# The second block's gates of tiles 4 to 7: pairs of weight tiles by seven quarter products

## The chip, the cores and the metric

The kernel runs on one core of one Trainium2 chip, in one launch. Time is the device time of that launch in microseconds. TensorE (PE), VectorE (DVE), ScalarE (ACT) and GpSimd (POOL) each work through a queue of their own in order; SyncE (SP) starts most DMAs.

## The reference, cut to what matters

The program computes two transformer blocks on 512 tokens of 1024 features, in float32. The first block is one layer with attention, a recurrence and a mixture of experts. The second block has two layers, each a mixing layer and a feed-forward stage. The change touches the mixing layer:

```
h = rmsnorm(x, norm_mix_g[l])
proj = einsum('bsd,de->bse', h, w_in[l])          # q, k, v, retention, convolution, gate_pre
...
gates = sigmoid(gate_pre + b_gate[l]).reshape(B, S, 3, D)
y = (gates[:, :, 0] * (o_da @ w_branch_da[l]) + gates[:, :, 1] * (o_ret @ w_branch_ret[l])
     + gates[:, :, 2] * (o_sc @ w_branch_sc[l]))
x = x + y @ w_out[l]
```

`gate_pre` has 3 x 1024 features, each a sum over the 1024 features of `h`. The feed-forward stage that follows is `x + (silu(conv(h @ w_g)) * (h @ w_u)) @ w_out`, with 2816 features in the middle.

## The kernel before, in words

**Numbers in two halves.** A float32 matrix product is made of three matmuls in the chip's faster rounded format. Each operand is split into a high half, a copy by ACT (`split`, line 953), and a low half, the difference that DVE takes; `mm3` (line 929) adds high x high, high x low and low x high in PSUM. So each weight that is loaded costs an ACT copy and a DVE subtraction before PE can use it, and each product three matmuls per 128 features.

**The plain product.** `mm_fm` (line 1106) makes 128 output features for all 512 tokens: the weight chunk of 1024 x 128 is loaded and split (`load_w`, line 974), and for each of 8 groups of 128 input features three matmuls of 512 columns (tokens) follow, 24 in all. With `halves=2` it does the tokens in two halves of 256 columns, 48 matmuls. `x` is what `norm_fm` (line 988) leaves: the normalized activations, transposed, features on partitions, split.

**The seven products.** The feed-forward stage has another way. `norm_quarters` (line 1007) leaves the same activations in quarters: two halves of the features by two halves of the tokens. `token_sums` (line 1037) forms four sums and differences of these quarters: four 1024-wide additions of high and low half on POOL, four 1024-wide additions or subtractions on DVE, and a split of each result (ACT and DVE). They stay in SBUF for the whole stage. `mm_seven` (line 1060) takes two weight tiles at once, forms four differences of their quarters on DVE, splits seven weight quarters, and makes both output tiles from seven products of a quarter by a quarter, where the direct way needs eight; each product is 4 x 3 matmuls of 256 columns. Results of products are copied out of PSUM (`ea`, `eb`, `ec`) between further products, and three additions on DVE put the outputs together.

**The mixing layer.** `mix2` (line 1874) normalizes, then projects q, k and v, then weaves the attention with the convolution branch (`sc2`, six plain products) and the retention's projections, then the retention with the gates of tiles 0 and 1. What is left runs tile by tile, here called the tail: for feature tile j the three gates that are still missing (one per branch b, plain products, with a tanh on ACT), then the three branch products and their sum, `y`. The output product `mm_tm_res` ends the layer. In 24 gate products per layer and the six of `sc2`, `x` is the moving operand of 512 columns; the projections use it as the stationary one, 128 tokens at a time.

**What sets the order.** The program is recorded first and then ordered by a planner (`Prog.order`, line 592). It fills each engine's queue in an order of its own, with costs of operations, room in SBUF and the program's order as the priority: an operation may stand well ahead of its place in the program where its inputs are there and room is free. SBUF is a few segments, `f` and `wf` for float32 and `r`, `wr` and at times `s` and `t` for the rounded format. With the program's `swing` in the mixing layer (line 1911), `t` becomes rounded too; `wr`, `r`, `s` and `t` then have 37120 columns. `SHARES` (line 2253) holds stretches of the program, by number of operation, where the planner sets part of the room aside.

In all profiles every instruction carries line 346, where the planner emits it; names are those of the segments, `bank` is a PSUM bank.

Of the kernel before, what the change touches and what calls it, by code (L numbers as in the profile page):

```python
# [16 lines left out]
AF = mybir.ActivationFunctionType  # L17
# [159 lines left out]
class Engine:  # L177


    def __init__(self, prog, name):  # L180
        self._p, self._n = prog, name
# [5 lines left out]
class Prog:  # L187
# [289 lines left out]
    def plan(self):  # L477
# [3 lines left out]
        deps, share = self.preds, np.ones(len(self.ops) + 1)  # L481
        for i, k in SHARES:
            share[max(0, i - 600):i + 100] -= 0.05 * k
# [418 lines left out]
                self.left[b.live][head:b.last + 1] += b.n  # L902


class Kernel:
    def __init__(self, p, a, out, dbg=None):
        self.p = self.nc = p
# [198 lines left out]
    def mm_fm(self, src, x, kts=8, halves=1):  # L1106

        w = self.load_w3(src, kts, P)
        ps = self.ps()
        n = S // halves  # L1110
        for h in range(halves):
            sl = slice(h * n, (h + 1) * n)
            for j in range(kts):
                self.mm3(ps[:, sl], (w[0][:, j, :], w[1][:, j, :]), (x[0][j][:, sl], x[1][j][:, sl]), j == 0, j == kts - 1)
        return ps
# [758 lines left out]
    def mix2(self, l):  # L1874
        nc, a = self.nc, self.a
        F = lambda name, shape: self.t(shape, F32, name)
        lam_init = 0.8 - 0.6 * math.exp(-0.3 * l)
        x = self.norm_fm(a[f"g_mix2{l}"], "h")
        vec = self.load(a[f"vec2{l}"], [P, NVEC2], "vec2")
        hb = F("hbg", (P, 24))  # L1880
        self.ts(hb, vec[:, L2_GATE:L2_GATE + 24], 0.5, OP.mult)
# [18 lines left out]
        gates = {}  # L1900

        def gate(*js):
            for j, b in js:
                ps = self.mm_fm(a[f"w_gate{l}"][8 * b + j], x)
                g = gates[j, b] = F("gate", (P, S))
                self.act(g, ps, AF.Tanh, scale=0.5, bias=hb[:, 8 * b + j:8 * b + j + 1])
                yield
        self.weave((ret, 240), (gate(*((j, b) for j in range(2) for b in range(3))), 160))
        tiles = lambda z, n: [[z[q][:, k, :] for k in range(n)] for q in range(2)]
        oda, ort, osc = tiles(oda, 4), tiles(ort, 2), [[osc[k][q][:, 0, :] for k in range(2)] for q in range(2)]  # L1910
        self.p.swing({"t": "R"})
        y = []
        for j in range(8):
            self.run_all(gate(*((j, b) for b in range(3) if (j, b) not in gates)))
            gt = [gates[j, b] for b in range(3)]
            for b, (w, o, kts) in enumerate((("w_bda", oda, 4), ("w_bret", ort, 2), ("w_bsc", osc, 2))):
                ps = self.mm_fm(a[f"{w}{l}"][j], o, kts)
                self.stt(gt[b], gt[b], 1.0, ps, OP.add, OP.mult)
            self.tt(gt[0], gt[0], gt[1], OP.add)
            self.tt(gt[0], gt[0], gt[2], OP.add)  # L1920
            yh, yl = self.t([P, S], R32, "yh"), self.t([P, S], R32, "yl")
            self.act(yh, gt[0], AF.Copy, scale=0.5)
            self.stt(yl, gt[0], 0.5, yh.bitcast(F32), OP.mult, OP.subtract)
            y.append((yh, yl))
# [325 lines left out]
SCRATCH = {"rel": [4, 640], "hx": [S, D], "fold0": [P, P], "fold1": [P, P], "fold2": [P, P], "fold3": [P, P]}  # L2250
GE = 4
GROUP, PLAIN = 4, 2
SHARES = ((3749, 1), (11237, 1), (14294, 1))


def build(nc, tc, a, out, dbg=None, stop=None, start=None):
# [18 lines left out]
```

## Time and profile before

| what | value |
|---|---|
| time, median of 3 runs | 2387.47 us (2382.23 to 2387.71) |
| profiled execution | 2380.74 us, its span 2379.0 us |
| busy in the span | PE 2277.1, PE weight loads 1803.6, DVE 1527.9, ACT 950.9, POOL 82.0 us |
| mixing layers of the second block | about 780 to 1200 us and 1570 to 2000 us |
| their tails (tiles 2 to 7 and the output product) | about 1045 to 1200 us and 1840 to 2000 us |
| feed-forward stages | about 1225 to 1570 us and 2020 to 2375 us |

A busy time of PE counts rows whose ends are modelled and overlap the next row, so PE can read busy and still not start matmuls as closely as it could; the distance between starts tells more. "Granted clock" is the share of TensorE's full clock that the chip allowed. A wait names the engine, and the segment it wrote, that came last before an instruction could start.

### The profile page before, as it was taken

The page shows a single profiled execution, that of the slowest core. Times are in us where ns is not written, and L with a number is a line of the kernel's source. Part 1 is how long each engine was busy: PE and PEld are TensorE (multiplying, and loading weights), DVE is VectorE, ACT ScalarE, POOL GpSimd, SP SyncE. Part 2 cuts the span into 40 slices and gives each one's busy share as a digit, 9 for nine tenths or more (in the row PEclk, how much of TensorE's full clock was granted, in tenths as well). Part 3 has the DMA queues.
Part 4 walks back from the last instruction along what each step waited for, and adds up shares of the span by engine and source line. Part 5 has one row for each costly group of instructions (what it writes and reads, how often), then busy time and mean ns, then how long its engine had stood idle before and what let it go on. Part 6 is the DMA issues. An engine that isn't in the chain of part 4 may idle for free.

```text
span 2379.0 us, 35153 instructions
## 1 busy us (share of the span) xinstructions
PE 2277.1 (96%) x13578; PEld 1803.6 (76%) x13578; DVE 1527.9 (64%) x3521; ACT 950.9 (40%) x1609; POOL 82.0 (3%) x107
## 2 busy tenths in 40 slices
PE   7999969899999899999999999999999999999999
PEld 6767647644444776778889999978777888999998
DVE  7876573533222957553579888776664446988885
ACT  5445422121311534333336555443442334555542
POOL 0100010000100000100010000000010000100000
PEclk9979987879999999999999999999999999999999
DMA  5002232379997321122413333332111332232231
GB/s 198 19 19 59 69 95 105 138 270 406 355 378 298 115 80 37 54 98 81 141 55 107 107 106 100 116 132 86 39 58 48 125 114 99 81 98 95 101 116 45
DMA packets 87425, 287.87 MB, mean 121 GB/s; under 512 B 11060, under 2 KB 16308, under 8 KB 87256
## 3 DMA queue, kind: packets, MB, share of 16 engines
q1 hardware_dynamic: 84376, 275.12, 33.1%
q0 software_dynamic: 2880, 10.49, 1.2%
q8 instruction: 107, 1.75, 0.3%
q14 instruction: 62, 0.51, 0.1%
HBM read 281.10 MB, written 4.47 MB: 120 GB/s over the span
## 4 chain that ended last, share of the span: by engine, by line
PE 83%; DVE 10%; DMA 3%; ACT 2%; issue 2%; POOL 0%; ACTq 0%; SPq 0%; DVEq 0%; POOLq 0%
PE bank L346 83%; DVE seg_f L346 3%; DVE seg_t L346 2%; DVE seg_tiny L346 2%; DVE seg_s L346 1%; DVE seg_wr L346 1%; DMA seg_wf<-in_w_o 1%; ACT seg_f L346 1%; DVE seg_r L346 1%; DMA seg_f<-in_w_ffi 0%; ACT seg_wr L346 0%; DMA seg_r<-in_w_moe 0%; DMA seg_t<-in_rot 0%; DVE seg_wf L346 0%; ACT seg_t L346 0%
## 5 line engine op out<-in xcount | busy, mean ns | idle before, releaser
L346 PE MATMUL bank<-seg_r,seg_wr 128*128 128x512 f32 (+1 forms) x1706 | 436.0, 352 | 0.6 <-DVE seg_wr L346 0.3
L346 PEld LDWEIGHTS bank<-seg_r,seg_wr 128*128 128x128 f32 x1706 | 290.6, 190 | 45.5 <-issue 1.4
L346 PE MATMUL bank<-seg_s,seg_wr 128*128 128x256 f32 (+1 forms) x1134 | 309.0, 327 | 0.0
L346 PE MATMUL bank<-seg_wr 128*128 128x512 f32 (+2 forms) x922 | 260.8, 389 | 4.3 <-DVE seg_wr L346 3.1
L346 ACT ACTIVATE seg_f<-bank 128x256 f32<-128x256 f32 (+5 forms) x313 | 135.7, 438 | 262.5 <-PE bank L346 238.2
L346 PE MATMUL bank<-seg_t,seg_wr 128*128 128x256 f32 (+1 forms) x1176 | 235.6, 283 | 0.4 <-ACT seg_t L346 0.4
L346 PE MATMUL bank<-seg_wr,seg_r 128*128 128x512 f32 (+1 forms) x748 | 230.1, 393 | 2.7 <-DVE seg_r L346 1.7
L346 ACT ACTIVATE seg_wr<-seg_f 128x1024 fp32r<-128x1024 f32 (+2 forms) x178 | 163.1, 923 | 135.5 <-PE bank L346 94.4
L346 PEld LDWEIGHTS bank<-seg_s,seg_wr 128*128 128x128 f32 x1134 | 195.7, 191 | 19.7 <-DVE seg_t L346 0.2
L346 PEld LDWEIGHTS bank<-seg_wr 128*128 128x128 f32 x922 | 170.9, 194 | 47.7 <-issue 6.9
L346 PE MATMUL bank<-seg_wr,seg_s 128*128 128x512 f32 x610 | 206.4, 394 | 0.5 <-DVE seg_f L346 0.5
L346 PEld LDWEIGHTS bank<-seg_t,seg_wr 128*128 128x128 f32 x1176 | 186.0, 190 | 1.7 <-ACT seg_t L346 0.6
L346 PE MATMUL bank<-seg_s 128*128 128x512 f32 (+4 forms) x672 | 180.4, 370 | 1.1 <-DVE seg_t L346 1.1
L346 PE MATMUL bank<-seg_r,seg_s 128*128 128x512 f32 (+2 forms) x548 | 174.2, 380 | 2.2 <-ACT seg_f L346 1.9
L346 DVE TENSOR_TENSOR seg_f<-bank,seg_f 128x512 f32<-128x512 f32 (+4 forms) x212 | 128.7, 613 | 72.5 <-PE bank L346 64.3
L346 DVE TENSOR_TENSOR seg_f<-seg_f 128x512 f32<-128x512 f32 (+5 forms) x271 | 158.1, 597 | 23.0 <-ACT seg_f L346 16.6
L346 ACT ACTIVATE seg_wr<-seg_wf 128x1024 fp32r<-128x1024 f32 (+4 forms) x118 | 113.1, 964 | 131.7 <-PE bank L346 93.4
L346 PEld LDWEIGHTS bank<-seg_wr,seg_r 128*128 128x128 f32 x748 | 137.9, 188 | 34.4 <-DVE seg_f L346 2.4
L346 PE MATMUL bank<-seg_s,seg_r 128*128 128x512 f32 (+3 forms) x502 | 160.7, 383 | 0.3 <-ACT seg_r L346 0.3
L346 PE MATMUL bank<-seg_t,seg_s 128*128 128x256 f32 (+7 forms) x566 | 128.2, 333 | 16.2 <-DVE seg_f L346 10.0
L346 PE MATMUL bank<-seg_f 128*128 128x128 f32 (+6 forms) x971 | 117.3, 279 | 27.1 <-DVE seg_f L346 22.4
L346 PE MATMUL bank<-seg_r 128*128 128x512 f32 (+2 forms) x426 | 140.0, 375 | 1.0 <-ACT seg_f L346 1.0
(340 smaller groups left out, 3834.4 us busy)
## 6 DMA issues: line engine op xcount, KB each, us to landing
seg_s<-in_w_moe SPq DMA_DIRECT2D x58, 512.0 KB, 10.1
seg_f<-in_w_ffi SPq DMA_DIRECT2D x52, 512.0 KB, 3.4
seg_f<-in_w_moe SPq DMA_DIRECT2D x42, 512.0 KB, 9.6
seg_r<-in_w_moe SPq DMA_DIRECT2D x42, 512.0 KB, 10.2
seg_wf<-in_w_ffi SPq DMA_DIRECT2D x36, 512.0 KB, 3.4
seg_t<-in_w_moe SPq DMA_DIRECT2D x33, 512.0 KB, 10.1
seg_f<-in_w_ffo SPq DMA_DIRECT2D x30, 512.0 KB, 3.2
seg_f<-in_w_gate SPq DMA_DIRECT2D x29, 512.0 KB, 3.9
```

Of the source, the lines that this page charges most:

```text
L346: return self.chain(eng, f(*[self.place_of(v) for v in a], **{n: self.place_of(v) for n, v in k.items()}))
```

## The change

The mixing layer takes its normalized activations from `norm_quarters` in place of `norm_fm`. A view, `Quarters`, shows the quarters as the eight feature groups that the old code expects; a slice of tokens must lie within one half, so `mm_fm` on such an `x` always works in halves of 256 columns. The gates of tiles 0 to 3 stay plain products. The gates of tiles 4 to 7 are made two tiles at a time by `mm_seven`, three calls (one per branch) for tiles 4 and 5 and three for 6 and 7, in each of the two layers; the tanh works in place on the two results. The token sums that this needs are made from the quarters after the `swing` in the program. `SHARES` has other entries.

```
+class Quarters:
+    def __getitem__(self, q):
+        return [Row([self.z[i][k // 4][q][:, k % 4, :] for i in range(2)]) for k in range(8)]
+class Row:
+    def __getitem__(self, at):
+        sl = at[1]
+        i = sl.start // 256
+        return self.halves[i][:, sl.start - 256 * i:sl.stop - 256 * i]
...
 def mm_fm(self, src, x, kts=8, halves=1):
     w = self.load_w3(src, kts, P)
     ps = self.ps()
+    halves = 2 if isinstance(x, Quarters) else halves
...
 def mix2(self, l):
-    x = self.norm_fm(a[f"g_mix2{l}"], "h")
+    z = self.norm_quarters(a[f"g_mix2{l}"], "h")
+    x = Quarters(z)
...
     self.p.swing({"t": "R"})
-    y = []
+    y, s = [], self.token_sums(z)
     for j in range(8):
-        self.run_all(gate(*((j, b) for b in range(3) if (j, b) not in gates)))
+        if j < 4:
+            self.run_all(gate(*((j, b) for b in range(3) if (j, b) not in gates)))
+        elif (j, 0) not in gates:
+            for b in range(3):
+                both = self.mm_seven([a[f"w_gate{l}"][8 * b + j + i] for i in range(2)], z, s)
+                for i, g in enumerate(both):
+                    self.act(g, g, AF.Tanh, scale=0.5, bias=hb[:, 8 * b + j + i:8 * b + j + i + 1])
+                    gates[j + i, b] = g
...
-SHARES = ((3749, 1), (11237, 1), (14294, 1))
+SHARES = ((3749, 1), (8121, 3), (14962, 1), (15802, 1))
```

`mm_seven`, which the feed-forward stage already calls, works on the two weight tiles so (left out are the loads and names):

```
for o, x, y in ((ta[:, :512], b12, b11), (ta[:, 512:], b22, ta[:, :512]), (tb[:, :512], b22, b12),
                (tb[:, 512:], b21, ta[:, 512:])):
    self.tt(o, x, y, OP.subtract)
...
product(pa[:, lo], w1, z[0][0], True, False)
self.act(ea[:, lo], pa[:, lo], AF.Copy)
product(pg[:, lo], w2, z[0][1], True, True)
product(ph[:, lo], t1, s1, True, False)
...
product(pg[:, hi], t4, z[1][1], True, True)
self.tt(ea, pg, ea, OP.add)
```

The order on the engines changes from the first mixing layer on; ahead of it both kernels stand alike. Three places follow.

On PE, in the first layer's tail, two gates of one tile stood behind each other before; `bank` is the PSUM bank written, what stands behind the arrow is the segments read, then columns and count:

```order
L346 MATMUL bank_89<-seg_r,seg_t 128x512 x2
L346 MATMUL bank_89<-seg_s,seg_t 128x512
L346 MATMUL bank_89<-seg_r,seg_t 128x512
L346 MATMUL bank_92<-seg_r,seg_wr 128x512 x13
L346 MATMUL bank_92<-seg_s,seg_wr 128x512
L346 MATMUL bank_92<-seg_r,seg_wr 128x512 x2
```

On PE at the first pair of tiles after the change, where the products of one call of seven end and the next call's begin:

```order
L346 MATMUL bank_91<-seg_r,seg_wr 128x256 x12
L346 MATMUL bank_88<-seg_s,seg_wr 128x256 x2
L346 MATMUL bank_92<-seg_s,seg_wr 128x256 x2
L346 MATMUL bank_89<-seg_s,seg_wr 128x256 x2
L346 MATMUL bank_87<-seg_wr 128x256 x2
L346 MATMUL bank_90<-seg_wr,seg_t 128x256 x2
L346 MATMUL bank_87<-seg_wr 128x256 x10
L346 MATMUL bank_89<-seg_s,seg_wr 128x256 x10
L346 MATMUL bank_88<-seg_s,seg_wr 128x256 x10
L346 MATMUL bank_92<-seg_s,seg_wr 128x256 x10
```

Matmuls of 512 columns gave way to runs of twelve with 256; at the start of a call several products begin with two matmuls each, those of the high half of the weight, and their other ten stand behind.

On DVE, in the first layer's opening, before: behind the norm of a query tile (`seg_tiny` rows) come low halves of weights (1024 columns into `seg_wr`):

```order
L346 TENSOR_TENSOR seg_t<-bank_93,seg_tiny 128x512
L346 TENSOR_TENSOR seg_t<-seg_t,seg_f 128x512
L346 TENSOR_REDUCE seg_tiny<-seg_f 128x8
L346 TENSOR_TENSOR seg_wr<-seg_wf,seg_s 128x1024
L346 TENSOR_SCALAR seg_tiny<-seg_tiny 128x8 x3
L346 SCALAR_TENSOR_TENSOR seg_tiny<-seg_tiny 128x8
L346 TENSOR_TENSOR seg_tiny<-seg_tiny 128x8
L346 TENSOR_TENSOR seg_wr<-seg_f,seg_s 128x1024 x2
```

On DVE at the same place, after:

```order
L346 TENSOR_TENSOR seg_wr<-seg_wf,seg_wr 128x1024
L346 SCALAR_TENSOR_TENSOR seg_tiny<-seg_tiny 128x8
L346 TENSOR_SCALAR seg_tiny<-seg_tiny 128x8
L346 TENSOR_TENSOR seg_wr<-seg_f,seg_wr 128x1024
L346 TENSOR_TENSOR seg_tiny<-seg_tiny 128x8
L346 TENSOR_SCALAR seg_tiny<-seg_tiny 128x8
L346 TENSOR_TENSOR seg_f<-seg_f,seg_wf 128x1024
L346 SCALAR_TENSOR_TENSOR seg_tiny<-seg_tiny 128x8 x2
L346 TENSOR_TENSOR seg_f<-seg_f 128x1024
```

The 1024-column operations that write `seg_f` are the token sums: with the low halves of a weight and of a sum they now stand between the small operations of the norms, some 1600 to 2000 operations ahead of their place in the program.

On DVE, in the second layer's tail at the gates of tile 6, before (1024 columns: low half of a gate's weight; `SCALAR_TENSOR_TENSOR` on a bank: a gate times a branch):

```order
L346 TENSOR_TENSOR seg_t<-seg_wf,seg_wr 128x1024
L346 TENSOR_TENSOR seg_wr<-seg_f,seg_s 128x1024
L346 SCALAR_TENSOR_TENSOR seg_f<-seg_f,bank_90 128x512
L346 SCALAR_TENSOR_TENSOR seg_f<-seg_f,bank_89 128x512
L346 TENSOR_TENSOR seg_wr<-seg_f,seg_t 128x1024
L346 SCALAR_TENSOR_TENSOR seg_wf<-seg_wf,bank_92 128x512
L346 TENSOR_TENSOR seg_f<-seg_f 128x512
L346 TENSOR_TENSOR seg_wr<-seg_f,seg_r 128x512
L346 TENSOR_TENSOR seg_f<-seg_f,seg_wf 128x512
```

On DVE at the same place, after:

```order
L346 TENSOR_TENSOR seg_f<-seg_f 128x512
L346 TENSOR_TENSOR seg_t<-seg_f,seg_wr 128x256
L346 TENSOR_TENSOR seg_f<-seg_wf,seg_f 128x512
L346 SCALAR_TENSOR_TENSOR seg_s<-seg_f,seg_r 128x512
L346 SCALAR_TENSOR_TENSOR seg_f<-seg_f,bank_91 128x512
L346 SCALAR_TENSOR_TENSOR seg_f<-seg_f,bank_90 128x512
L346 TENSOR_TENSOR seg_f<-seg_wf,seg_f 128x512
L346 SCALAR_TENSOR_TENSOR seg_f<-seg_f,bank_86 128x512
L346 TENSOR_TENSOR seg_f<-seg_f 128x512
L346 TENSOR_TENSOR seg_wr<-seg_f,seg_wr 128x1024
L346 TENSOR_TENSOR seg_f<-seg_f 128x512
L346 TENSOR_TENSOR seg_wr<-seg_f,seg_wr 128x1024
```

The first 1024-column row is the low half that the first product of tiles 6 and 7 reads. The rows ahead of it are the last low halves of tile 5's branches, the gating of tiles 4 and 5, and the weights' differences (`seg_f<-seg_wf,seg_f`).

## Rows read from the trace of the kernel before

**Rows 1.** the page, busy time, share of the span, instructions by engine
```profile
PE 2277.1 (96%) x13578; PEld 1803.6 (76%) x13578; DVE 1527.9 (64%) x3521; ACT 950.9 (40%) x1609; POOL 82.0 (3%) x107
```

**Rows 2.** the page, the chain that ended last, by engine
```profile
PE 83%; DVE 10%; DMA 3%; ACT 2%; issue 2%; POOL 0%; ACTq 0%; SPq 0%; DVEq 0%; POOLq 0%
```

**Rows 3.** stretches: two mixing tails and a feed-forward stage (columns first)
```profile
core 0: us, PE busy (x) PEld busy (x) DVE busy (x) ACT busy (x) POOL busy (x), PEclk, DMA share, GB/s
1100.00:1150.00 50.00, 50.00 (x217) 40.30 (x216) 17.59 (x25) 14.82 (x22) 0.00 (x0) 1.00 0.27 85
1850.00:1900.00 50.00, 50.00 (x218) 40.36 (x217) 18.75 (x26) 17.89 (x26) 0.00 (x0) 1.00 0.34 110
1400.00:1450.00 50.00, 50.00 (x360) 47.08 (x358) 42.37 (x60) 28.88 (x42) 0.00 (x0) 1.00 0.26 86
```

**Rows 4.** waits of PE, 755 to 1200 us: total, times, longest (us)
```profile
PE bank L346 <- DVE seg_t L346: 8.5, 2, 7.9
PE bank L346 <- DVE seg_f L346: 0.9, 1, 0.9
```

**Rows 5.** PE in order of time, narrow matmuls: start, length, operation, count
```profile
1313.36 1.59 PE L346 MATMUL bank<-seg_t,seg_wr 128*128 128x256 f32 x12
1314.79 0.28 PE L346 MATMUL bank<-seg_s,seg_wr 128*128 128x256 f32 x1
```

**Rows 6.** DVE by form, 1200 to 2379 us: count, busy us, mean ns
```profile
L346 DVE TENSOR_TENSOR seg_f<-seg_f 128x512 f32<-128x512 f32 x144 | 98.8, 693 | 8.8 <-ACT seg_f L346 5.3 <-DMA seg_f<-in_w_ffi 2.4
...
L346 DVE TENSOR_TENSOR seg_wr<-seg_f,seg_wr 128x1024 fp32r<-128x1024 f32 x48 | 58.6, 1221 | 11.8 <-PE bank L346 11.3 <-ACT seg_f L346 0.3
...
L346 DVE TENSOR_TENSOR seg_f<-seg_f 128x256 f32<-128x256 f32 x42 | 17.7, 421 | 10.4 <-ACT seg_f L346 10.3
L346 DVE TENSOR_TENSOR seg_f<-bank,seg_f 128x256 f32<-128x256 f32 x42 | 17.5, 419 | 5.6 <-PE bank L346 5.0 <-ACT seg_f L346 0.5
...
L346 DVE SCALAR_TENSOR_TENSOR seg_f<-seg_f,bank 128x512 f32<-128x512 f32 x23 | 15.2, 680 | 0.0
L346 DVE TENSOR_TENSOR seg_wr<-seg_f,seg_wr 128x512 fp32r<-128x512 f32 x21 | 14.4, 687 | 4.8 <-ACT seg_wr L346 2.8 <-PE bank L346 1.9
```

**Rows 7.** the page, transfers of the gates' weights: count, size, us to landing
```profile
seg_f<-in_w_gate SPq DMA_DIRECT2D x29, 512.0 KB, 3.9
```

**Rows 8.** POOL in order of time in the two feed-forward openings
```profile
1243.33 2.84 POOL L346 TENSOR_TENSOR seg_f<-seg_r 128x1024 f32<-128x1024 f32 x1 [4.35 <-issue]
...
2035.04 2.40 POOL L346 TENSOR_TENSOR seg_f<-seg_r 128x1024 f32<-128x1024 f32 x1 [10.30 <-issue]
```

**Rows 9.** DVE by form beside the POOL sums, 1228 to 1262 us
```profile
L346 DVE TENSOR_TENSOR seg_wf<-seg_f 128x512 f32<-128x512 f32 x2 | 4.4, 2198 | 0.0
...
L346 DVE TENSOR_TENSOR seg_f<-seg_f,seg_wf 128x1024 f32<-128x1024 f32 x1 | 3.2, 3239 | 0.1
```

**Rows 10.** stretches, the openings of the two mixing layers
```profile
780.00:850.00 70.00, 62.10 (x293) 50.99 (x292) 62.88 (x199) 31.53 (x46) 0.00 (x0) 0.95 0.32 107
1570.00:1650.00 80.00, 79.96 (x372) 63.53 (x371) 62.44 (x201) 32.52 (x50) 0.00 (x0) 1.00 0.27 93
```

**Rows 11.** stretches, the openings of the two feed-forward stages
```profile
1200.00:1250.00 50.00, 49.05 (x300) 43.41 (x299) 42.79 (x91) 16.93 (x26) 9.19 (x4) 1.00 0.13 43
1250.00:1300.00 50.00, 47.89 (x385) 47.38 (x384) 49.06 (x64) 35.96 (x54) 1.78 (x1) 0.97 0.32 106
2000.00:2050.00 50.00, 48.66 (x331) 44.59 (x330) 42.41 (x84) 21.72 (x31) 9.56 (x4) 1.00 0.10 33
2050.00:2100.00 50.00, 47.12 (x354) 44.88 (x353) 48.23 (x70) 30.82 (x49) 0.00 (x0) 1.00 0.39 127
```

**Rows 12.** stretches with a lower granted clock (column PEclk)
```profile
1000.00:1040.00 40.00, 40.00 (x199) 31.40 (x199) 14.50 (x54) 8.87 (x23) 0.00 (x0) 0.91 0.16 50
1800.00:1820.00 20.00, 20.00 (x94) 15.84 (x93) 8.76 (x37) 3.98 (x13) 0.00 (x0) 0.83 0.08 27
```

More of the change, by code (lines that the diff above doesn't have):

```diff
@@ L902, in end, with __init__ @@
                 self.left[b.live][head:b.last + 1] += b.n
+class Quarters:
+    def __init__(self, z):
+        self.z = z
+    def __getitem__(self, q):
+        return [Row([self.z[i][k // 4][q][:, k % 4, :] for i in range(2)]) for k in range(8)]
+class Row:
+    def __init__(self, halves):
+        self.halves = halves
+    def __getitem__(self, at):
+        sl = at[1]
+        i = sl.start // 256
+        return self.halves[i][:, sl.start - 256 * i:sl.stop - 256 * i]
 class Kernel:
@@ L1908, in mix2 @@
         self.weave((ret, 240), (gate(*((j, b) for j in range(2) for b in range(3))), 160))
-        tiles = lambda z, n: [[z[q][:, k, :] for k in range(n)] for q in range(2)]
+        tiles = lambda v, n: [[v[q][:, k, :] for k in range(n)] for q in range(2)]
         oda, ort, osc = tiles(oda, 4), tiles(ort, 2), [[osc[k][q][:, 0, :] for k in range(2)] for q in range(2)]
         self.p.swing({"t": "R"})
-        y = []
+        y, s = [], self.token_sums(z)
         for j in range(8):
-            self.run_all(gate(*((j, b) for b in range(3) if (j, b) not in gates)))
+            if j < 4:
[6 more added lines that the diff above has]
+                        gates[j + i, b] = g
             gt = [gates[j, b] for b in range(3)]
```

## The prediction

> **What bounds the kernel now.** I read the page's busy shares first, then its chain of waits, then the stretches of the second block, then PE's own waits there. PE is busy 2277.1 of 2379.0 us, DVE 1527.9 [rows 1], and 83% of the chain that ended last is PE [rows 2]. The stretches say where that holds. In the tail of a mixing layer, where the gates of tiles 2 to 7 stand, PE is busy in all 50 of 50 us while DVE has 17.59 or 18.75 us of work; in the feed-forward stage, which uses the seven products already, PE is also busy throughout, but DVE has 42.37 of 50 [rows 3]. So in the tail a microsecond of PE work is a microsecond of time, and DVE has room. The one large wait of PE in the first mixing layer, 7.9 us on DVE, is at its opening [rows 4]. The same normalization stands there afterwards, so I leave that wait in.
>
> **PE's work.** A busy PE row overlaps the next, so I price by starts. In the tail 217 matmuls, all 512 columns wide, start in 50 us: 0.2304 us each [rows 3]. Twelve 256-column matmuls start between 1313.36 and 1314.79: 0.1192 us each [rows 5]. Half the columns thus cost 0.0040 us more than half the time.
> - Twelve calls of the seven products (two pairs of tiles, three branches, two layers) each take the place of two plain products. Before: 2 x 24 x 0.2304 = 11.06 us. After: 7 x 4 x 3 = 84 matmuls x 0.1192 = 10.01 us. Gain 1.05 us, twelve times: 12.6 us.
> - The plain products that stay (in each layer six of the convolution branch, twelve gates) find the tokens in halves and issue 48 narrow matmuls for 24 wide ones: 5.72 against 5.53 us, 0.19 us more, 36 times: 6.8 us lost.
> - Projections, attention, retention, branch products and the output product keep their matmuls.
>
> Net on PE: 12.6 - 6.8 = 5.8 us gained, 0.24% of the time. That is nearly all there is to gain, and everything else goes against it.
>
> **DVE's work in tiles 4 to 7.** A seven issues on DVE four 512-wide subtractions (0.69 each), low halves of 1024 columns three times (1.22) and of 512 once (0.69), and three additions after the products (0.42, 0.42, 0.69): 8.6 us, where two plain weights took 2.4 [rows 6]. A tile's branches take 0.69 + 0.42 + 0.42 of low halves, 3 x 0.68, 2 x 0.69 and 0.69 = 5.6 us as before. For two tiles DVE then has 3 x 8.6 + 2 x 5.6 = 37.0 us, PE 3 x 10.01 + 2 x 24 x 0.2304 = 41.1 us: 90%. Before it was 2 x (3 x 1.22 + 5.6) = 18.5 of 44.2 us, 42%. The feed-forward stage runs PE without a gap at 85% [rows 3], so 90% need not bound, but the work is not spread evenly. The third excerpt of the order shows it: the low half that the first product of tiles 6 and 7 needs stands behind nine other DVE instructions; the ten take 7.1 us by their rows, and beside them PE's queue holds 16 wide and 4 narrow matmuls, 4.2 us. PE then has only the high half's matmuls to run, as the pairs of x2 in the first excerpt show, and waits; queued behind the waiting matmul are all later ones, since PE takes them in order. If DVE has run ahead, the wait is nothing; if it has not, 2.9 us, and the worst opening of the feed-forward stage lost 4.2 us. There are four such starts. I take 1.1 us each, nearer to the steady feed-forward rows than to its openings: 4.4 us, between 0 and 16.8.
>
> ACT has 28.88 of 50 us in the feed-forward stretch [rows 3], with the same sevens, and stays free. The gate weights are the same transfers, 3.9 us to land [rows 7], loaded ahead; with them stands no price.
>
> **The token sums.** Each mixing layer gets four 1024-wide sums of high and low half on POOL, four subtractions or additions and four low halves on DVE: 8 x 1.22 = 9.8 us on DVE. The second excerpt shows that the order puts them into the opening, between the head norms and the weights of the projections, not into the slack tail. POOL takes 2.40 us for one, or 2.84 [rows 8]. Beside them DVE slows: two 512-wide subtractions took 2.198 us instead of 0.69, one 1024-wide addition 3.239 instead of 1.22 [rows 9]. A POOL sum so costs DVE between 0 and 2.0 us, four of them 0 to 8.1; I take half, for only some of DVE's work has two operands in SBUF, and have 13.8 us of DVE per layer. In the first layer's opening DVE is busy 62.88 of 70 us, in the second's 62.44 of 80 [rows 10]. So 7.1 and 17.6 us are free: the first overruns by 6.7 us, the second doesn't. An overrun reaches PE only where a head norm or a weight is due: PE's transposes of q and k stand in its queue behind those norms. The nearest rows are the feed-forward openings, where the same sums come and the sevens begin: PE lost 0.95 + 2.11 = 3.1 us in one and 1.34 + 2.88 = 4.2 in the other [rows 11]. I take 3 us for the first layer and 1 for the second: 4 us, between 0 and 10.9 (6.7 and 4.2).
>
> The Trainium skill says more against the change (SBUF — State Buffer, section "SBUF: two separate sides"): GpSimd and VectorE share one port pair as an exclusive lock, and an operation with two SBUF inputs blocks fully against a GpSimd operation that reads SBUF. The lengthened rows agree with it. By that rule every POOL sum would hold DVE for its whole length; what this makes of the time is the fourth rival.
>
> **The sum.** 5.8 gained, 4.4 + 4.0 lost: 2.6 us slower than the profiled execution, which took 2380.74 us (span 2379.0 and 1.7 around it). That execution lies 6.7 us under the median of the three runs (2387.47, from 2382.23 to 2387.71), so the forecast for the median is 2390 us, 0.1% above before. A measurement of this kernel can tell about 0.3%, some 7 us, from no change.
>
> **Rivals.**
> 1. *All of the new DVE work is hidden.* For it: 42.37 of 50 in the feed-forward stage costs PE nothing. Against it: both feed-forward openings lose time on DVE. 2387.5 - 5.8 = 2382 us.
> 2. *The changed order also removes the slow clock.* Between 1000 and 1040 us and between 1800 and 1820 the granted clock is 0.91 and 0.83 on average [rows 12], which is time at the lower of the two levels: 40 x 0.09 + 20 x 0.17 = 7 us of full-speed work. PE there runs the retention's small matmuls among gate products, and these become narrower and move. If half the loss goes and the DVE work is hidden: 2378 us. Nothing in the change aims at it, and the loss can grow as well.
> 3. *DVE becomes the bound in tiles 4 to 7.* Token quarters and sums hold 16384 columns of the rounded kind, the branch outputs 8192, the finished tiles 6144 by tile 6; of 37120 columns 6400 are left, and one seven's weight parts want 7168. Then weights can't be prepared ahead, and every start of a pair pays the feed-forward's worst opening. 4 x 4.2 = 16.8 in place of 4.4, with the openings as forecast: 2387.5 - 5.8 + 16.8 + 4 = 2402 us, slower. It decides once DVE's 37.0 us for a pair, with the waits for room, exceed PE's 41.1. Against it: the feed-forward keeps PE full with 85% on DVE.
> 4. *POOL holds DVE fully.* Four sums of 2.40 to 2.84 us block 9.6 to 11.4 us; with 9.8 us of work the first opening overruns by up to 14.1 us and the second by up to 3.6. All of it on PE: 2387.5 - 5.8 + 17.7 + 4.4 = 2404 us. Against it: only a few of the rows near POOL's are lengthened.
>
> **How the numbers follow.** Forecast 45% (own range 2383 to 2398; a tenth of all lies above 2394.6, 0.02 under 2380.3), the first rival 25% (2377 to 2386, 0.10 of it faster by over 0.3%), the second 5%, faster, the third 17%, slower, the fourth 8%, of which 0.07 slower. Faster 0.17, within 0.3% 0.49, slower 0.34. The range leaves out a tenth on each side: 2378 to 2402.
>
> **What would show it.** In the profile after: some 1296 more matmul records (36 x 24 more, and 12 x 36 more from the sevens), narrow ones 0.119 us apart also in the mixing layers, 217 per 50 us gone from the tail; DVE's busy sum up by about 12 x 6.2 + 2 x 9.8 = 94 us, and more where POOL runs beside it; DVE near 45 of 50 in tiles 4 to 7 with PE's waits on DVE at the starts of the pairs, and longer DVE rows in the two openings. The forecast is wrong if the mixing layers show gaps of PE of over 15 us together that are not there before, or no new ones at all; if narrow matmuls start more than 0.13 us apart there; or if stretches at the lower clock come or go.

## The result and the profile after

The changed kernel takes 2401.34 us (median of 6 runs, 2398.01 to 2406.95) against 2386.26 us before (6 runs on the same chip, 2380.32 to 2390.23): ratio 1.0067, 95% interval 1.0055 to 1.0080. It is 0.67% slower, about 15 us. The forecast was 2390 us, 2.6 over before: the right sign, a sixth of the size. 2401 lies just inside the range, near the third rival (2402) and the fourth (2404).

The page of the changed kernel, its busy times and its chain, against [rows 1, 2]:

```profile
PE 2277.5 (95%) x14874; PEld 1873.6 (78%) x14874; DVE 1623.2 (68%) x3645; ACT 990.7 (41%) x1689; POOL 103.3 (4%) x115
...
PE 75%; DVE 16%; DMA 4%; ACT 2%; issue 2%; POOL 0%; SPq 0%; ACTq 0%; DVEq 0%; POOLq 0%
```

There are 1296 more matmuls, as counted, and DVE has 95.3 us more, with what POOL lengthens in it (94 forecast, without). But PE's busy sum has not fallen, and DVE's share of the chain is 16% where it was 10%. From the first transposes of layer 0 to the end it takes 1607.7 us where it took 1588.9 (2399.7 - 791.98 and 2379.0 - 790.11): 18.8 us more. Where PE stands still is read from the stretches that answer to [rows 10, 3] (opening of layer 0, of layer 1, the second half of each tail; columns as there):

```profile
core 0: us, PE busy (x) PEld busy (x) DVE busy (x) ACT busy (x) POOL busy (x), PEclk, DMA share, GB/s
780.00:850.00 70.00, 56.35 (x264) 45.72 (x264) 67.64 (x184) 31.14 (x44) 10.92 (x4) 0.95 0.20 66
1570.00:1650.00 80.00, 74.15 (x319) 58.71 (x318) 66.42 (x167) 28.71 (x43) 10.52 (x4) 0.94 0.17 59
1100.00:1150.00 50.00, 46.28 (x319) 41.79 (x318) 37.26 (x55) 23.99 (x39) 0.00 (x0) 1.00 0.29 87
1150.00:1200.00 50.00, 48.03 (x317) 43.91 (x317) 39.67 (x56) 28.73 (x44) 0.00 (x0) 0.97 0.48 148
1900.00:1950.00 50.00, 49.58 (x350) 46.26 (x348) 36.55 (x56) 23.86 (x39) 0.00 (x0) 1.00 0.32 101
1950.00:2000.00 50.00, 48.82 (x323) 45.28 (x324) 41.05 (x57) 30.43 (x46) 0.00 (x0) 0.97 0.43 143
```

In the openings PE lacks 13.65 and 5.85 us of work where it lacked 7.90 and 0.04: two new gaps of 5.8 us. The tails, full before, lack 5.69 and 1.60 in these rows, 6.3 and 2.7 in all of 1000 to 1200 and 1800 to 2000 us. These gaps, 11.6 and 9.0 us, are more than the whole loss. The prediction had named gaps of over 15 us together as a sign that it is wrong. POOL's 10.9 and 10.5 us in the openings are the token sums. DVE with POOL beside it, in order of time, layer 0 (start, length, operation; POOL's rows first, DVE's below, rows between left out):

```profile
797.44 5.72 POOL L346 TENSOR_TENSOR seg_f<-seg_s 128x1024 f32<-128x1024 f32 x2 [177.04 <-DMA seg_wf<-in_w_qkv]
812.13 2.40 POOL L346 TENSOR_TENSOR seg_f<-seg_s 128x1024 f32<-128x1024 f32 x1 [8.96 <-DVE seg_s L346]
814.49 2.84 POOL L346 TENSOR_TENSOR seg_wf<-seg_s 128x1024 f32<-128x1024 f32 x1
```

```profile
797.87 3.06 DVE L346 SCALAR_TENSOR_TENSOR seg_t<-seg_wf,seg_tiny,seg_f 128x1024 f32<-128x1024 f32 x1
...
800.92 3.33 DVE L346 TENSOR_TENSOR seg_r<-seg_t,seg_r 128x1024 fp32r<-128x1024 f32 x1
...
804.25 1.21 DVE L346 TENSOR_TENSOR seg_r<-seg_wf,seg_r 128x1024 fp32r<-128x1024 f32 x1
...
812.57 0.68 DVE L346 TENSOR_TENSOR seg_t<-bank,seg_tiny 128x512 f32<-128x512 f32 x1
813.16 0.67 DVE L346 TENSOR_REDUCE seg_tiny<-seg_t 128x8 f32<-128x512 f32 x1
813.76 1.32 DVE L346 TENSOR_TENSOR seg_t<-seg_t,seg_f 128x512 f32<-128x512 f32 x1
815.00 2.77 DVE L346 TENSOR_SCALAR seg_tiny<-seg_tiny 128x8 f32<-128x8 f32 x3
```

The 1024-wide operations that meet POOL's first two sums take 3.06 and 3.33 us; the next like one, at 804.25 when POOL is idle, takes 1.21. The 512-wide one at 813.76 takes 1.32 (0.69 elsewhere). Three operations on eight columns (0.17 each elsewhere) take 2.77: they get done as POOL's last sum ends. Those that read a PSUM bank or reduce one operand keep 0.68 and 0.67. Each sum has one such lengthened row. In layer 1 they are these, the first on a single column (0.15 us elsewhere):

```profile
1603.42 2.04 DVE L346 SCALAR_TENSOR_TENSOR seg_tiny<-seg_tiny 128x1 f32<-128x1 f32 x1
...
1605.38 3.44 DVE L346 SCALAR_TENSOR_TENSOR seg_wf<-seg_wf,seg_tiny,seg_f 128x1024 f32<-128x1024 f32 x1
...
1616.88 1.25 DVE L346 TENSOR_SCALAR seg_tiny<-seg_tiny 128x8 f32<-128x8 f32 x1
...
1619.18 2.36 DVE L346 TENSOR_SCALAR seg_tiny<-seg_tiny 128x8 int32<-128x8 int32 x1
```

Against the same operations elsewhere the rows are longer by 6.7 us in layer 0 and 7.3 in layer 1, 1.8 us a sum. In layer 0 PE's transposes wait behind just these chains, the norm of the next 128 tokens and the head norms (in brackets the wait):

```profile
800.99 1.10 PE L346 MATMUL bank<-seg_f,seg_t 128*128 128x128 f32 x8 [0.97 <-DVE seg_tiny L346]
...
809.71 1.09 PE L346 MATMUL bank<-seg_f,seg_t 128*128 128x128 f32 x8 [1.92 <-DVE seg_t L346]
...
815.13 0.66 PE L346 MATMUL bank<-seg_f,seg_t 128*128 128x128 f32 x4 [0.45 <-DVE seg_t L346]
...
820.51 1.39 PE L346 MATMUL bank<-seg_wr,seg_s 128*128 128x512 f32 x5 [2.41 <-DVE seg_t L346]
```

0.97 + 1.92 + 0.45 + 2.41 = 5.75 us, the whole new gap of this opening. In layer 1 two waits make it, 3.4 and 2.5 us, and the first is followed by the lower clock (columns as above; in the second row PE has worked 1.62 of 5 us):

```profile
1600.00:1605.00 5.00, 5.00 (x25) 3.80 (x24) 4.93 (x18) 2.68 (x7) 1.96 (x1) 1.00 0.01 3
1605.00:1610.00 5.00, 1.62 (x9) 1.19 (x8) 4.83 (x8) 0.00 (x0) 2.74 (x2) 0.75 0.00 0
1610.00:1615.00 5.00, 5.00 (x20) 4.27 (x20) 2.28 (x4) 1.90 (x4) 0.00 (x0) 0.57 0.28 105
```

One remark on comparing: the second block begins at other times in other runs (PE's first transposes of layer 0, behind the 7.9 us wait, at 790.11 before, at 791.98 after, up to 799.50 in the experiments, whatever the kernel). So the table below has, beside the times, the time from those transposes to the span's end, and its two parts: the two mixing layers, from the first transposes of a layer's norm to those of the feed-forward stage, and the two feed-forward stages. These come from one execution each. After the change the mixing layers are 15.0 us longer; the feed-forward stages, which it leaves as they are, are 3.8 us longer. One operation parts the queues before the mixing layer, contrary to what I wrote: a small fill on POOL, at 165 us before the change.

### The profile page after: what moved, and what is told of

The parts are those of the page before. It is cut to its first block, busy times and chain, and to the rows that moved or that the text cites. A ratio compares the mean times of both kernels' runs of the same rounds, so it can differ in the third digit from the quotient of the medians.

```text
span 2399.7 us, 38030 instructions
## 1 busy us (share of the span) xinstructions
PE 2277.5 (95%) x14874; PEld 1873.6 (78%) x14874; DVE 1623.2 (68%) x3645; ACT 990.7 (41%) x1689; POOL 103.3 (4%) x115
## 3 DMA queue, kind: packets, MB, share of 16 engines
q8 instruction: 117, 1.92, 0.3%
## 4 chain that ended last, share of the span: by engine, by line
PE 75%; DVE 16%; DMA 4%; ACT 2%; issue 2%; POOL 0%; SPq 0%; ACTq 0%; DVEq 0%; POOLq 0%
PE bank L346 75%; DVE seg_f L346 5%; DVE seg_tiny L346 3%; DVE seg_t L346 2%; DVE seg_wr L346 2%; DVE seg_s L346 2%; DVE seg_r L346 1%; ACT seg_f L346 1%; DVE seg_wf L346 1%; ACT seg_wr L346 1%; DMA seg_f<-in_w_ffi 1%; DMA seg_wf<-in_w_o 0%; ACT seg_t L346 0%; DMA seg_wf<-in_w_ffi 0%; DMA fold<-seg_f 0%
## 5 line engine op out<-in xcount | busy, mean ns | idle before, releaser
L346 PE MATMUL bank<-seg_r,seg_wr 128*128 128x256 f32 (+1 forms) x1855 | 386.7, 316 | 6.5 <-DVE seg_r L346 2.5
L346 PEld LDWEIGHTS bank<-seg_s,seg_wr 128*128 128x128 f32 x1945 | 301.8, 192 | 13.5 <-DVE seg_wr L346 4.8
L346 PE MATMUL bank<-seg_wr 128*128 128x512 f32 (+3 forms) x1110 | 293.7, 365 | 4.5 <-DVE seg_wr L346 1.8
L346 PE MATMUL bank<-seg_wr,seg_s 128*128 128x512 f32 (+1 forms) x780 | 229.0, 388 | 3.8 <-DVE seg_t L346 2.4
L346 ACT ACTIVATE seg_f<-bank 128x256 f32<-128x256 f32 (+6 forms) x332 | 140.0, 426 | 218.6 <-PE bank L346 203.5
L346 PE MATMUL bank<-seg_t,seg_wr 128*128 128x256 f32 x940 | 195.1, 283 | 0.6 <-ACT seg_f L346 0.4
L346 DVE TENSOR_TENSOR seg_f<-seg_f 128x512 f32<-128x512 f32 (+6 forms) x292 | 173.5, 609 | 28.9 <-ACT seg_f L346 23.4
L346 PEld LDWEIGHTS bank<-seg_wr,seg_s 128*128 128x128 f32 x780 | 143.7, 188 | 35.3 <-issue 2.8
L346 DVE TENSOR_TENSOR seg_wr<-seg_f,seg_wr 128x1024 fp32r<-128x1024 f32 (+2 forms) x124 | 126.7, 1023 | 49.6 <-PE bank L346 39.1
L346 PE MATMUL bank<-seg_s,seg_r 128*128 128x256 f32 (+3 forms) x586 | 152.0, 352 | 0.6 <-ACT seg_r L346 0.3
L346 PE MATMUL bank<-seg_s 128*128 128x256 f32 (+4 forms) x581 | 142.1, 354 | 1.1 <-DVE seg_t L346 1.1
## 6 DMA issues: line engine op xcount, KB each, us to landing
seg_s<-in_w_moe SPq DMA_DIRECT2D x58, 512.0 KB, 10.2
seg_r<-in_w_moe SPq DMA_DIRECT2D x42, 512.0 KB, 10.2
seg_t<-in_w_moe SPq DMA_DIRECT2D x33, 512.0 KB, 10.2
```

The costliest lines, as they stand in the source:

```text
L346: return self.chain(eng, f(*[self.place_of(v) for v in a], **{n: self.place_of(v) for n, v in k.items()}))
```

## The experiments

Theory 1a: POOL's sums hold DVE, and PE pays. 1b: DVE's own added work is what PE waits for. 2: the loss is made in tiles 4 to 7. The ratio is that of a kernel's time to the kernel before on the same chip; the columns behind it are from one profile each, all in us.

| kernel | median us | ratio, 95% interval | from transposes, us | mixing layers | feed-forward | DVE busy | POOL busy |
|---|---|---|---|---|---|---|---|
| before | 2386.26 | | 1588.9 | 872.8 | 716.1 | 1527.9 | 82.0 |
| after | 2401.34 | 1.0067, 1.0055 to 1.0080 | 1607.7 | 887.8 | 719.9 | 1623.2 | 103.3 |
| 1 sums late | 2397.31 | 1.0061, 1.0045 to 1.0077 | 1604.2 | 883.5 | 720.7 | 1623.4 | 104.6 |
| 2 sums on DVE | 2383.06 | 0.9994, 0.9983 to 1.0004 | 1587.5 | 864.4 | 723.1 | 1612.9 | 84.2 |
| 3 halves alone | 2385.21 | 0.9997, 0.9985 to 1.0009 | 1587.5 | 867.0 | 720.4 | 1526.5 | 85.3 |
| 4 POOL sums in before | 2399.48 | 1.0062, 1.0044 to 1.0080 | 1601.6 | 885.6 | 716.0 | 1545.3 | 101.1 |
| 5 no sums | 2389.39 | 1.0014, 1.0000 to 1.0027 | 1589.6 | 852.9 | 736.6 | 1592.6 | 83.3 |
| 6 all sums on DVE | 2370.15 | 0.9938, 0.9917 to 0.9959 | 1573.4 | 862.3 | 711.1 | 1607.5 | 62.9 |
| 7 before, FF sums on DVE | 2381.94 | 0.9978, 0.9966 to 0.9991 | 1582.9 | 872.2 | 710.7 | 1529.8 | 60.5 |
| 8 wide and spread | 2377.86 | 0.9964, 0.9951 to 0.9977 | 1583.9 | 867.5 | 716.4 | 1624.4 | 65.9 |
| 9 halves in the tail | 2392.00 | 1.0028, 1.0013 to 1.0042 | 1596.6 | 875.3 | 721.3 | 1526.2 | 81.9 |
| 10 halves in the weave | 2375.35 | 0.9955, 0.9938 to 0.9973 | 1585.5 | 862.6 | 722.9 | 1526.1 | 84.8 |
| 11 fills on POOL | 2382.59 | 0.9984, 0.9970 to 0.9998 | 1589.4 | 872.8 | 716.6 | 1531.5 | 88.4 |
| 12 before with both | 2372.10 | 0.9947, 0.9929 to 0.9964 | 1571.3 | 857.4 | 713.8 | 1524.9 | 63.2 |

**1. The sums later.** A dependence on the retention's result holds them back.

```
 self.tt(o, flat(z[i][h][0]).bitcast(F32), flat(z[i][h][1]).bitcast(F32), OP.add, eng=nc.gpsimd)
+if late is not None:
+    self.p.ops[-1].reads.append(self.p.touch(late))      # late = ort[1][1]
```

> The changed kernel with its token sums held back until the retention is finished, so that they stand at the start of the tail and not in the mixing layer's opening. Theory 1 (the sums in the opening make DVE late, and PE waits there: 11.6 us of new gaps, and a lower clock after them): the openings look as before the change, the tail takes the sums on, and the time falls from 2401 to 2386-2394 us. Theory 2 (the loss is made in tiles 4 to 7, where DVE is the bound): the time stays at 2398 us or more, and the gaps in the tails grow.

Theory 1 as I had put it did not come out. The openings are clean again (7.9 us of wait in the first, 1.0 in the second), yet the time stays, within 1 us of what theory 2 asked for, and the tails' gaps grow. But they grow where the sums now stand, at the start of the tail, with a lower clock behind the wait:

```profile
1000.00:1050.00 50.00, 44.65 (x283) 40.83 (x282) 26.45 (x66) 10.77 (x23) 7.01 (x3) 0.84 0.07 22
```

PE lacks 5.35 us in these 50 while DVE is busy only 26.45. It is one wait. Three sums on POOL meet three operations on four columns, of 0.16 us each, in a chain that PE waits for (POOL's row first, DVE's, then PE's):

```profile
1009.27 7.01 POOL L346 TENSOR_TENSOR seg_f<-seg_s 128x1024 f32<-128x1024 f32 x3 [47.14 <-ACT seg_r L346]
```

```profile
1009.24 2.45 DVE L346 SCALAR_TENSOR_TENSOR seg_tiny<-seg_tiny 128x4 f32<-128x4 f32 x2
1011.73 2.28 DVE L346 TENSOR_TENSOR seg_tiny<-seg_tiny 128x4 f32<-128x4 f32 x1
1014.04 2.26 DVE L346 SCALAR_TENSOR_TENSOR seg_tiny<-seg_tiny 128x4 f32<-128x4 f32 x1
```

```profile
1017.83 0.66 PE L346 MATMUL bank<-seg_f 128*128 128x128 f32 x2 [5.35 <-DVE seg_f L346]
```

So the place alone is not the cause: the loss went where the sums went.

**2. The sums on DVE.** `eng=nc.vector` for the mixing layers' sums; the rest as after.

> The changed kernel with the four sums of high and low half on DVE in place of POOL, in the same place: 4.9 us more work for DVE per layer, none on POOL beside it. If POOL's operations hold DVE for most of their length (theory 1a: about 1.7 us each, 7 us per layer), DVE ends no later than before and the gaps of PE in the two openings stay at 11.6 us or shrink to 8: 2396 to 2402 us. If it is DVE's own added work that makes it late and POOL does nothing to it (theory 1b), 4.9 us more per layer go to PE's waits: about 2408 to 2411 us.

2383 us, better than theory 1a promised and far from 1b's 2408. PE waits 7.9 us in the first opening, as before the change, and not at all from 1560 to 1650 us, though DVE has 9.8 us more of its own work in all (8 x 1.22). The two openings:

```profile
780.00:850.00 70.00, 62.10 (x295) 51.52 (x294) 68.98 (x210) 32.93 (x47) 0.00 (x0) 0.95 0.26 81
1570.00:1650.00 80.00, 80.00 (x375) 64.30 (x374) 70.16 (x210) 32.71 (x49) 0.00 (x0) 1.00 0.20 66
```

DVE is busier there than after the change (68.98 against 67.64, 70.16 against 66.42), and PE has no new gap. Over the whole span DVE's busy sum even falls, from 1623.2 to 1612.9, so POOL had lengthened DVE's work by 10.3 + 9.8 = 20.1 us. The rows beside the sums account for 14.0 of that; busy sums of kernels with the same work on DVE lie some 5 us apart (1526.2 in experiment 9, 1531.5 in 11), so the rows are the better measure.

**4. POOL's sums alone, in the kernel before.**

```
 self.p.swing({"t": "R"})
+for i, h in ((0, 0), (1, 0), (1, 1), (0, 1)):
+    v = [zs[h][q][:, :, 256 * i:256 * i + 256].bitcast(F32) for q in range(2)]
+    self.tt(F("za", (P, 1024)).rearrange("p (k t) -> p k t", k=4), *v, OP.add, eng=nc.gpsimd)
```

> The kernel before the change with four additions of 1024 columns on POOL in each mixing layer's opening, of high and low half of the activations, whose results nothing reads. Nothing is added on DVE, ACT or PE. Theory 1a (POOL holds DVE): DVE's rows beside the four get about 7 us longer per layer, PE waits 2 to 5 us in each opening: 2390 to 2396 us. Theory 1b (only DVE's own work counts): as before, 2386 us within 2.

Eight additions that nobody reads cost as much as the whole change: 1.0062, above the 2390 to 2396 us of theory 1a. The openings:

```profile
780.00:850.00 70.00, 56.01 (x254) 44.90 (x253) 62.19 (x172) 29.12 (x43) 10.85 (x4) 0.93 0.28 96
1570.00:1650.00 80.00, 74.82 (x336) 58.93 (x336) 66.61 (x175) 29.23 (x45) 9.53 (x4) 0.98 0.24 84
```

PE lacks 13.99 and 5.18 us, as after the change, though DVE is busy no longer than before in the first (62.19 against 62.88). DVE's busy sum rises by 17.4 us over the whole span; the lengthened rows beside the eight sums add up to 14.8. This and experiment 2 settle 1a against 1b; and 2 falls as the cause of the loss, for the sevens are in experiment 2 and absent here.

**11. Fills in place of sums.**

```
-    self.tt(F("za", (P, 1024)).rearrange("p (k t) -> p k t", k=4), *v, OP.add, eng=nc.gpsimd)
+    o = F("za", (P, 1024))
+    nc.gpsimd.memset(o, 0.0)
+    self.p.ops[-1].reads.append(self.p.touch(zs[h][1][:, :, 256 * i:256 * i + 256]))
```

> The kernel before with four fills of 1024 columns with zero on POOL in each mixing layer's opening, in the place where the run with additions had those (they follow the same quarters by a dependence, and read nothing from SBUF). If it is POOL's reading that holds DVE, DVE's rows keep their lengths and the time is that of before, 2384 to 2389 us. If any POOL instruction holds DVE, it is slower by its length, up to 2395 us.

No loss (2383 us, 1 us under the expected range). The same DVE operations, first beside the additions of experiment 4, then, the two wide ones, beside the fills:

```profile
800.20 3.04 DVE L346 SCALAR_TENSOR_TENSOR seg_t<-seg_wf,seg_tiny,seg_f 128x1024 f32<-128x1024 f32 x1
...
803.23 3.34 DVE L346 TENSOR_TENSOR seg_s<-seg_t,seg_r 128x1024 fp32r<-128x1024 f32 x1
...
817.40 2.78 DVE L346 TENSOR_SCALAR seg_tiny<-seg_tiny 128x8 f32<-128x8 f32 x3
```

```profile
802.96 1.27 DVE L346 SCALAR_TENSOR_TENSOR seg_t<-seg_wf,seg_tiny,seg_f 128x1024 f32<-128x1024 f32 x1
...
804.22 1.22 DVE L346 TENSOR_TENSOR seg_s<-seg_t,seg_r 128x1024 fp32r<-128x1024 f32 x1
...
815.54 0.57 DVE L346 TENSOR_SCALAR seg_tiny<-seg_tiny 128x8 f32<-128x8 f32 x3
```

The last row met no fill. Three fills stood in a row (801.96 to 804.95), and no row beside them is longer, so an operation with two operands in SBUF is not held by a fill. Operations on eight columns with one operand are: in layer 1 each of the two rows below has one (0.17 us elsewhere) that ends as a fill ends (POOL's fills behind them):

```profile
1602.21 1.18 DVE L346 TENSOR_SCALAR seg_tiny<-seg_tiny 128x8 f32<-128x8 f32 x2
...
1603.73 0.67 DVE L346 TENSOR_SCALAR seg_tiny<-seg_tiny 128x8 int32<-128x8 int32 x1
```

```profile
1602.41 1.97 POOL L346 MEMSET seg_f<- 128x1024 f32 x2 [6.10 <-DVE seg_tiny L346]
```

A fill takes POOL 0.95 us, an addition 2.4, so the time of this run does not tell reading from length by itself; the rows do, for operations with two operands.

**5. No sums.** `s = (z[0][0], z[0][1], z[1][0], z[1][1])`.

> The changed kernel without the token sums of the mixing layers: the products of seven take four of the quarters in their place, so this part of the computation is left out, and nothing else. It prices the sums whole. With POOL's hold as the loss (theory 1a) the sums on DVE (2383 us in the run before) are hidden in the opening, and this kernel takes the same, 2380 to 2384 us. If the sums' own 14.7 us of DVE per layer also cost, it comes below 2378 us. If the gaps in the tails come from the sums, they go; by the excerpt of the order (the low half that the first product reads stands behind nine others) they stay at 7 to 9 us in all.

Inconclusive on the time: 2389 us, more than with the sums on DVE. The order differs in the first feed-forward opening, where PE now lacks 9.8 us (41.92 + 48.32 of 100 busy), a loss in a stage whose sums are still made. From the last step of layer 1's norm on it is 8 us faster than experiment 2 (1604.47 to 2385.7 us against 1590.21 to 2379.4). On the tails it is plain: PE lacks only 1.3 and 0.5 us there (1000 to 1200 and 1800 to 2000 us), with the same sevens. So the tails' gaps hang on the sums too: by their work, by the room in SBUF that they hold, or by the order that the planner makes with them. What the sums cost on DVE is left open: the mixing layers are 11.5 us shorter than in experiment 2, the feed-forward stages 13.5 longer.

**6 and 7. All sums on DVE, after and before the change.** `eng=nc.gpsimd` goes from `token_sums`, so that the feed-forward stages' sums move as well. `SHARES` had to be adjusted, so the planner's room differs as well; what that alone does was not tried.

> The changed kernel with all token sums on DVE, those of the two feed-forward stages too (SHARES adjusted, since the program's room is tight). If POOL holds DVE wherever it stands (theory 1a), the feed-forward openings, where DVE is busy 49 of 50 us, gain per sum the hold less the work, 2.4 - 1.2 us, eight times some 10 us: 2373 to 2379 us. If POOL's hold mattered only beside the norms, the time stays at 2381 to 2385 us.

> The kernel before the change with the feed-forward stages' token sums on DVE (SHARES adjusted). By theory 1a the same 10 us as in the run beside it: 2375 to 2380 us. By the other reading no change: 2384 to 2387 us.

Both gain. Experiment 6 beats both kernels, by 0.62% and by some 1.3%. Experiment 7 gains 5 us of the 10 expected, experiment 6 13 us over experiment 2, more than expected. Its feed-forward openings, in the stretches of [rows 11]:

```profile
1200.00:1250.00 50.00, 50.00 (x338) 45.93 (x337) 38.74 (x84) 19.20 (x29) 0.00 (x0) 1.00 0.04 11
1250.00:1300.00 50.00, 46.86 (x350) 44.00 (x349) 47.28 (x67) 31.86 (x50) 0.00 (x0) 1.00 0.42 138
2000.00:2050.00 50.00, 49.78 (x378) 47.34 (x377) 43.78 (x83) 26.25 (x40) 0.00 (x0) 1.00 0.14 43
2050.00:2100.00 50.00, 48.60 (x364) 46.24 (x363) 47.62 (x70) 28.69 (x46) 0.00 (x0) 1.00 0.35 117
```

PE lacks 3.14 us in the first two rows and 1.62 in the last two; in [rows 11] 3.06 and 4.22, with the sums of experiment 2 (still on POOL there) 3.94 and 4.29. That is 3.5 us of the 13. Another 3.7 us are gaps in the first tail (1050 to 1200 us: 4.70 us lacking in experiment 2, 1.01 here), where the order changed too. By stages, 12.0 of the 14.1 us between the two profiles lie in the feed-forward stages, and 5.4 of the 6.0 that experiment 7 gains over the kernel before. That 7 gains less than expected fits the rows: a sum on POOL held DVE by 1.5 us in the feed-forward openings before (rows longer by 6.0 us in the first, 5.9 in the second), so DVE saves 0.3 us a sum there and not 1.2.

**3, 9, 10. The halves.** Experiment 3 is the changed kernel with all gates plain (`if j < 8`, no sums). 9 and 10 take the kernel before and set `halves=2` in `mm_fm`, for the gates of tiles 2 to 7, or for the convolution branch and the gates of tiles 0 and 1.

> The changed kernel with the quarters and their view, all gates as plain products, no products of seven and no token sums. It prices the halves alone: 60 plain products of 48 narrow matmuls in place of 24 wide ones, 0.19 us each, 11.4 us over the kernel before: 2397 to 2399 us if nothing else changes. If the narrower matmuls cost nothing where PE's loads hide, about 2386 us. No theory expects new gaps in the openings.

> The kernel before with the tokens in two halves of 256 columns for the gates of tiles 2 to 7 alone (18 products a layer; the activations lie as before, the places in SHARES moved by the operations added). By the spacing of narrow matmuls it costs 36 x 0.19 = 6.8 us: 2393 to 2395 us if nothing else changes. If halves are free wherever they stand, 2386 us.

> The same for the other twelve products of a layer, those woven with the attention and the retention (the convolution branch and the gates of tiles 0 and 1). By the spacing 24 x 0.19 = 4.6 us: 2390 to 2392 us. The run with halves in all 30 came out level with the kernel before instead of 11.4 us above it; if what pays for them lies in the weave (narrower matmuls between the small ones of attention and retention), this kernel is faster than before, 2375 to 2382 us, and the one with halves in the tail is not.

In the tail the price of the time is as worked out, +0.28%, 6.7 us for 36 products (6.8 expected). That is in part luck: in the profile 2.5 us more lie in the mixing layers, where the lower clock at the start of layer 1's tail went, and 5.2 in the feed-forward stages. In the weave 24 products with halves make the kernel faster by 0.45%, 10.7 us, where 4.6 us of loss were expected. Experiment 3 has both, 6.7 - 10.7 = -4 us by these two; it measured -0.7 (-3.6 to 2.1). Why the weave gains is open. In the profiled run of 10, the slowest of its six, the time from the transposes is only 3.4 us less than before: the mixing layers gain 10.2 us, the feed-forward stages lose 6.8. No single wait accounts for it. Experiment 3's mixing layers are 5.8 us shorter than before, its feed-forward stages 4.3 longer.

**8 and 12. Two more versions.** 8 (its edit shortened here): all sums on DVE, both token halves in one tile so that plain products stay 512 wide, and sevens for two of three gates in tiles 2 to 7. 12: the kernel before with 7 and 10 together. Both have `SHARES` of their own.

```
+full = [self.pair(4, name) for _ in range(2)]
+z = [[[full[h][q][:, :, 256 * i:256 * i + 256] for q in range(2)] for h in range(2)] for i in range(2)]
...
-            if j < 4:
-                self.run_all(gate(*((j, b) for b in range(3) if (j, b) not in gates)))
-            elif (j, 0) not in gates:
-                for b in range(3):
+            self.run_all(gate(*((j, b) for b in (range(3) if j < 2 else (0,)) if (j, b) not in gates)))
+            if j >= 2 and (j, 1) not in gates:
+                for b in range(1, 3):
```

> The best version that the runs point to: all token sums on DVE; the quarters kept as halves of one tile, so that the plain products keep 512 columns; and the products of seven for two of the three gates of tiles 2 to 7 in place of all three of tiles 4 to 7 (as many as before, spread out, so that a pair of tiles has 30.8 us of DVE beside 42.1 of PE). If the halves cost 0.19 us each as their spacing says, and the tails' gaps come from DVE's uneven work, it gains 6.8 us and some 6 us over the kernel with all sums on DVE: 2362 to 2371 us. If the halves are free, as the run with halves alone suggests, and the gaps stay, no gain over it: 2373 to 2379 us.

> The kernel before the change, with no products of seven in the mixing layers, but with the two things that the runs found to gain: the feed-forward stages' token sums on DVE, and halves of 256 columns for the twelve woven products of a layer (SHARES adjusted). If the two gains add up (0.22% and 0.45%), 2386 - 5.3 - 10.7 = 2370 us, level with the changed kernel with all sums on DVE (2370), and the products of seven in the mixing layer themselves bring nothing. If the sevens carry part of that kernel's gain, this one stays above 2374 us.

8 is 0.36% faster than before and behind 6. That widening the woven products takes away what experiment 10 found would fit, but 8 differs in the sevens and in `SHARES` as well, so it is not shown; the tails still have gaps of 3 to 4 us each. 12, without sevens in the mixing layers, is level with 6 (0.9947 and 0.9938, intervals that overlap).

## Why the prediction was wrong

- **The step that failed** is in "The token sums", in two places. The first: "A POOL sum so costs DVE between 0 and 2.0 us, four of them 0 to 8.1; I take half, for only some of DVE's work has two operands in SBUF". By its rows a sum costs DVE 1.8 us (14.0 / 8 after the change) to 1.9 (14.8 / 8, experiment 4), so four cost 6.7 and 7.3 us where I took 4.0. The few lengthened rows of [rows 9] had misled me: one held operation carries most of a POOL row, so few are enough. Operations with one operand in SBUF are held as well (2.77 us for three on eight columns).
- The second place weighs more: "7.1 and 17.6 us are free: the first overruns by 6.7 us, the second doesn't". Room summed over 70 or 80 us does not help a norm that is held just when PE's transposes wait for it: with 68.98 us of DVE in the first opening PE had no new gap (experiment 2), with 62.19 and POOL beside it 6.1 us (experiment 4). Both layers lost 5.8 us, and the second paid some 5.1 us of full-speed work more at the lower clock (PEclk by 5 us: 0.75, 0.57, 0.80 and 0.86 behind the two waits), some of it while PE waited anyway. Forecast for the openings 4.0, within 0 to 10.9; measured 11.6 and the clock. The effect of the sums on POOL in place of DVE is 1.0067 against 0.9994, some 17 us.
- The fourth rival had the mechanism, with a chance of 8%, and came to 2404, near by luck. It put 14.1 us on the first layer and 3.6 on the second, since it too counted free room in the second; 5.8 and 5.8 came, and the clock. The rule of the Trainium skill (SBUF — State Buffer, section "SBUF: two separate sides") that I weighed there says that whichever of the two starts first holds the port pair for its whole instruction. The rows agree, both ways round: DVE's 3.06 and 3.33 in layer 0, and POOL's own row in layer 1 (the lower of the two rows under this point) that began just behind a DVE operation (the upper) and took 3.47 us instead of 2.4. The rule should have had the larger chance: the one 1024-wide row that I had of it, 3.239 for 1.22, is a hold of 2.0 us beside POOL's 2.84.

```profile
1618.04 1.21 DVE L346 TENSOR_TENSOR seg_wr<-seg_wf,seg_wr 128x1024 fp32r<-128x1024 f32 x1
```

```profile
1618.05 3.47 POOL L346 TENSOR_TENSOR seg_f<-seg_s,seg_wr 128x1024 f32<-128x1024 f32 x1
```

- The starts of the sevens: 4.4 forecast (0 to 16.8), 9.0 us of gaps in the two tails after, 8.1 with the sums on DVE. The sign is right, the size doubled, the place right in part: after the change the largest gaps, 1.20 us at 1114.80 and 1.15 and 0.68 at 1148.53 and 1149.71, stand in front of matmuls of calls of seven, others (0.60, 1.05) in front of 512-wide ones. The reason that I gave is not shown, for without the sums 1.9 us are left (experiment 5). DVE did not become the bound: it has 36.55 to 41.05 of 50 us there, so the third rival did not happen as a bound, though its number fits. Its reason, that weights find no room beside the sums, experiment 5 leaves standing.
- PE's work. Narrow matmuls start 0.120 us apart in the mixing layer (144 in 17.26 us), and the sevens issue what was counted. The halves' 6.8 us fail for the woven products: there, in the kernel before, they gained 10.7 us where 4.6 of loss stood. The losses beyond the forecast (7.6 us of gaps and some 5.1 of clock in the openings, 4.6 in the tails, 3.8 in the feed-forward stages) add up to 21 us, and the profile is 16 beyond it, so some gain hid a part of them; the woven halves may be it.
- The second rival: the dips moved. The one in layer 0's tail grew (granted 0.84, 0.50 and 0.98 in the three 10 us from 1000 on), that in layer 1's tail went, and the one in layer 1's opening came.

With the sums on DVE the change is worth 0.9994 of the kernel before. The parts do not add up to that: 12.6 us forecast for the sevens and 10.7 for the woven halves, less 2.3 for the halves in the tail and 8.1 for the gaps, would be a gain of 12.9, and 1.4 came. In the profile the mixing layers gain 8.4 us and the feed-forward stages, which the change leaves as they are, lose 7.0; why those lose is open. Nor is a gain of the sevens to be seen in the time: experiment 3, halves without sevens, is as fast (0.9997), its mixing layers 2.6 us longer, and 12, without sevens, is as fast as 6.

## What to carry to other kernels

Before an elementwise operation goes to POOL, look at what DVE does beside it: count up to POOL's whole row as DVE time unless DVE's operations there read PSUM, and ask which engine waits for the one that is held, however short it is. A stage's average slack is no cover for work that is put into a chain PE waits on. And price a split of matmuls where it stands: the same halves cost some 6 us in a full tail and gained in a weave of small matmuls.

## What the runs showed of the hardware

- An addition on POOL with its operands in SBUF holds a DVE operation until POOL's row ends, however small that operation is: one on a single column took 2.04 us in place of 0.15, one with a single operand on eight columns 2.36 in place of 0.17. Operations that read a PSUM bank or reduce keep their length (0.68, 0.67).
- A fill on POOL does not hold operations with two operands in SBUF (1.27 and 1.22 us beside fills, 3.04 and 3.34 beside additions), but it does hold ones with a single operand on eight columns (0.67 in place of 0.17).
- A wait of PE of 3.4 us was followed by 0.57 of full clock over the next 5 us of full work, so the wait is not all that it costs.
